# Split SiLU-multiply on one core: the first tile's store in four pieces, and no copy ahead of the third load

## The chip, the cores and the metric

The kernel runs on one core of a Trainium2 chip. Its time is device time in microseconds (us), as the median of several runs; less is better. Beside the times there is one profiled execution with a trace of every instruction and every DMA packet. The engines that matter here are ScalarE (ACT), VectorE (DVE), SyncE (SP, which only issues transfers) and the core's 16 DMA engines, which move data between HBM and the on-chip memory (SBUF, 128 partitions).

## The reference

```python
batch, seq, dim = (32, 512, 2048)          # x: float32
half_dim = x.shape[-1] // 2
x1, x2 = x[..., :half_dim], x[..., half_dim:]
silu_x1 = x1 * (1 / (1 + np.exp(-x1)))
return (silu_x1 * x2).astype(np.float32)   # (32, 512, 1024)
```

Each of the 16384 rows of 2048 numbers becomes one row of 1024: SiLU of the left half times the right half. 134 MB are read and 67 MB written.

## The kernel before

The 16384 rows are cut into 16 tiles of 1024 rows. A tile gives each of the 128 partitions `K` = 8 neighbouring rows, so a partition's share of a load is 64 KB in one stretch of HBM, and its share of a store is 32 KB. The input tiles `xt` and the output tiles `ot` come from pools with two buffers each: tile i + 2 has the buffers of tile i.

One tile is worked on in four chunks of `KC` = 2 rows. For each chunk ACT writes SiLU of the left half to `ot` (line 87), and DVE multiplies `ot` in place by the right half (line 92).

The schedule is written out by hand, so each engine does its instructions in program order:

- ACT issues the loads (line 74) as well as computing. Loads 0 and 1 come first (the first one is moved ahead of the opening barrier). After the four chunks of tile i ACT issues load i + 2, which waits until ACT and DVE have read tile i, since it overwrites that buffer. Tile i + 1's activations stand behind that load in ACT's queue.
- SP issues the stores. Tiles 0 to 14 are stored whole, when their last multiply is done (line 100). The last tile, 15, is stored in four pieces of two rows, each when its multiply is done (line 98).
- DVE does the multiplies, and once, after tile 0, a copy of one row of `xt` onto itself (line 103). Load 2 overwrites that buffer, so it waits for the copy too, while the store of tile 0 only waits for the last multiply.

An activation of tile i + 2 writes to the buffer that the store of tile i reads, so it waits for that store. The program's framework places the semaphores for these waits.

Of the kernel before, what the change touches and what calls it, by code (L numbers as in the profile page):

```python
# [1 line left out]

# [4 lines left out]


def issue_ahead_of_the_first_barrier(nc):

    head, body = nc.main_func.blocks[:2]
    load = next(ins for ins in body.instructions if type(ins).__name__ == "InstDMACopy")
    at = next(
        j for j, ins in enumerate(head.instructions)
        if ins.engine == load.engine and type(ins).__name__ == "InstDrain"
    )
    body.instructions = [ins for ins in body.instructions if ins.name != load.name]  # L20
    head.instructions = head.instructions[:at] + [load] + head.instructions[at:]


@with_exitstack
def kernel(
    ctx: ExitStack,
    tc: tile.TileContext,
    x: bass.AP,
    out: bass.AP,
):  # L30

    nc = tc.nc
    P = nc.NUM_PARTITIONS

    x_flat = x.flatten_outer_dims()  # L40
    out_flat = out.flatten_outer_dims()
    num_rows, in_cols = x_flat.shape
    half = in_cols // 2
    dt = x_flat.dtype

    K = 8
    KC = 2
    PLAN = [K] * (num_rows // (P * K))

    in_pool = ctx.enter_context(tc.tile_pool(name="in_pool", bufs=2))  # L50
    out_pool = ctx.enter_context(tc.tile_pool(name="out_pool", bufs=2))

    plan = []
    row = 0
    for k in PLAN:
        plan.append((row, k))
        row += P * k
    assert row == num_rows
    n_tiles = len(plan)

    def view(flat, i):
        row0, k = plan[i]
        return flat[row0:row0 + P * k].rearrange("(p k) d -> p k d", k=k)

    nc.at_finalize(issue_ahead_of_the_first_barrier)


    ctx.enter_context(tc.manual_schedule())

    loaded = {}  # L70

    def load(i):
        xt = in_pool.tile([P, K, in_cols], dt, name="xt")
        nc.scalar.dma_start(out=xt[:, :plan[i][1], :], in_=view(x_flat, i))
        loaded[i] = xt

    load(0)
    load(1)
    for i in range(n_tiles):
        k = plan[i][1]  # L80
        xt = loaded.pop(i)
        last = i == n_tiles - 1
        ov = view(out_flat, i)
        ot = out_pool.tile([P, K, half], dt, name="ot")
        for c in range(0, k, KC):
            ce = min(c + KC, k)
            nc.scalar.activation(  # L87
                out=ot[:, c:ce, :],
                in_=xt[:, c:ce, :half],
                func=mybir.ActivationFunctionType.Silu,  # L90
            )
            nc.vector.tensor_mul(  # L92
                out=ot[:, c:ce, :],
                in0=ot[:, c:ce, :],
                in1=xt[:, c:ce, half:],
            )
            if last:
                nc.sync.dma_start(out=ov[:, c:ce, :], in_=ot[:, c:ce, :])
        if not last:
            nc.sync.dma_start(out=ov, in_=ot[:, :k, :])  # L100
        if i == 0:

            nc.vector.tensor_copy(out=xt[:, k - 1, :half], in_=xt[:, k - 1, :half])  # L103
        if i + 2 < n_tiles:
            load(i + 2)


# [1 line left out]
_INS = ['x']  # L109
_OUTS = [((32, 512, 1024), 'float32')]  # L110


# [23 lines left out]
```

## Time and profile before

| | us |
|---|---|
| median of 3 runs | 470.83 (470.68 to 471.1) |
| the profiled execution: its time | 470.83 |
| the profiled execution: its span | 469.0 |
| DVE busy (64 multiplies and the copy) | 142.9 |
| ACT busy (64 activations, a table load) | 118.2 |

The span is the stretch that the instructions cover; 1.8 us of the time lie around it. Of a profile's lines: a group reads "line, engine, operation, written tile <- read tiles, shape, how many"; in the list by time the first number is the start in us from the span's start, the second the length, and brackets hold how long the engine had been idle and what ended that. `ACTq`, `DVEq` and `SPq` are the engines' issuing sides, at which semaphore waits and transfers stand. In the row of 40 slices, one digit is the busy share of 11.7 us in tenths. q10 is the queue of ACT's transfers (the loads), q1 that of SP's (the stores).

### The profile page before, as it was taken

To read this page: it belongs to the slowest core of one execution; us is meant where nothing else is said; L and a number is where in the kernel's file an instruction comes from. 1 tells how busy PE (TensorE), PEld (TensorE's weight loads), DVE (VectorE), ACT (ScalarE), POOL (GpSimd) and SP (SyncE) were. 2 spreads that over 40 slices of the span, in tenths; PEclk is the share of its full clock that TensorE was granted. 3 is DMA by queue.
4 is the path that set the end of the run, shared out by engine and by line. 5 is a ranking of instruction groups with operands and counts; after the bars stand their busy time and mean duration, and the time that the engine had idled before them with its cause. 6 is when DMAs were issued, how large, how long until landed. Compare 5 with 4: busy or idle time off the path is not lost.

```text
span 469.0 us, 271 instructions
## 1 busy us (share of the span) xinstructions
DVE 142.9 (30%) x65; ACT 118.2 (25%) x65; POOL 0.2 (0%) x4
## 2 busy tenths in 40 slices
DVE  0080705207051060611606015070250702407033
ACT  1151406014060230602306032060420604106050
POOL 0000000000000000000000000000000000000000
DMA  9899999999999998999999999999999999999998
GB/s 425 386 442 402 436 458 442 408 411 439 447 447 402 444 472 380 447 481 397 464 400 430 467 442 408 408 442 447 447 402 442 464 391 447 439 433 469 397 413 353
DMA packets 5042, 201.35 MB, mean 429 GB/s; under 512 B 560, under 2 KB 560, under 8 KB 560
## 3 DMA queue, kind: packets, MB, share of 16 engines
q10 hardware_dynamic: 2304, 134.22, 66.4%
q1 hardware_dynamic: 2736, 67.11, 33.2%
q14 instruction: 2, 0.02, 0.0%
HBM read 134.22 MB, written 67.11 MB: 429 GB/s over the span
## 4 chain that ended last, share of the span: by engine, by line
DMA 80%; DVE 15%; ACT 3%; DVEq 0%; issue 0%
DMA xt<-in_x_dram 80%; DVE ot L92 15%; ACT ot L87 3%; DVEq L131 0%
## 5 line engine op out<-in xcount | busy, mean ns | idle before, releaser
L92 DVE TENSOR_TENSOR ot<-ot,xt 128x2048 f32<-128x2048 f32 x64 | 142.3, 2286 | 319.1 <-ACT ot L87 319.1
L87 ACT ACTIVATE ot<-xt 128x2048 f32<-128x2048 f32 x64 | 116.9, 1897 | 339.0 <-DMA xt<-in_x_dram 339.0
L87 ACT ACT_TABLE_LOAD x1 | 1.3, 1283 | 1.3 <-PEq L120 1.3
L103 DVE COPY xt<-xt 128x1024 f32<-128x1024 f32 x1 | 0.7, 683 | 0.0
L120 POOL MEMSET const-bfloat16-1.0<- 128x1 bf16 x1 | 0.1, 101 | 0.0
L120 POOL MEMSET const-uint8-127<- 128x1 uint8 x1 | 0.1, 101 | 0.0
L120 POOL MEMSET const-float32-0.0<- 128x1 f32 x1 | 0.1, 98 | 0.2 <-issue 0.2
L120 POOL MEMSET const-float32-1.0<- 128x1 f32 x1 | 0.1, 98 | 0.0
## 6 DMA issues: line engine op xcount, KB each, us to landing
out_dram<-ot SPq DMA_DIRECT2D x15, 4096.0 KB, 39.7
out_dram<-ot SPq DMA_DIRECT2D x4, 1024.0 KB, 5.7
xt<-in_x_dram ACTq DMA_DIRECT2D x16, 47.1
```

What stands on the lines that cost most here:

```text
L87: nc.scalar.activation(out=ot[:, c:ce, :], in_=xt[:, c:ce, :half], func=mybir.ActivationFunctionType.Silu,)
L92: nc.vector.tensor_mul(out=ot[:, c:ce, :], in0=ot[:, c:ce, :], in1=xt[:, c:ce, half:],)
L103: nc.vector.tensor_copy(out=xt[:, k - 1, :half], in_=xt[:, k - 1, :half])
L120: nc = _bacc.Bacc("TRN2", target_bir_lowering=False, num_devices=1)
```

## The change

The first tile is now stored like the last one: each two-row piece as soon as its multiply is done. The copy on DVE is gone, so load 2 waits for tile 0's last multiply alone. Nothing else differs.

```diff
     for i in range(n_tiles):
         k = plan[i][1]
         xt = loaded.pop(i)
-        last = i == n_tiles - 1
+        in_pieces = i in (0, n_tiles - 1)
         ov = view(out_flat, i)
         ot = out_pool.tile([P, K, half], dt, name="ot")
         for c in range(0, k, KC):
...
-            if last:
+            if in_pieces:
                 nc.sync.dma_start(out=ov[:, c:ce, :], in_=ot[:, c:ce, :])
-        if not last:
+        if not in_pieces:
             nc.sync.dma_start(out=ov, in_=ot[:, :k, :])
-        if i == 0:
-
-            nc.vector.tensor_copy(out=xt[:, k - 1, :half], in_=xt[:, k - 1, :half])
         if i + 2 < n_tiles:
             load(i + 2)
```

## The prediction

> **What bounds the kernel now.** I read the page first (slices, queues, chain), then the issues with their landing times, then the start in order of time, and last the packet records behind section 3.
>
> ```profile
> DMA  9899999999999998999999999999999999999998
> q10 hardware_dynamic: 2304, 134.22, 66.4%
> q1 hardware_dynamic: 2736, 67.11, 33.2%
> DMA 80%; DVE 15%; ACT 3%; DVEq 0%; issue 0%
> out_dram<-ot SPq DMA_DIRECT2D x15, 4096.0 KB, 39.7
> out_dram<-ot SPq DMA_DIRECT2D x4, 1024.0 KB, 5.7
> xt<-in_x_dram ACTq DMA_DIRECT2D x16, 47.1
> ```
>
> The 16 DMA engines are busy in every slice, and the loads (q10) and stores (q1) together take 66.4% + 33.2% = 99.6% of their time. The chain names loads, DVE and ACT in turn, but each of its steps only issues a transfer into engines that are full already. So the time is the sum of the packets, plus any moment in which both queues are empty.
>
> The packet records say what one engine does. A load gives each engine eight packets of 64 KB at 2418 ns and a completion; a whole store gives eight of 32 KB at 1213 ns; a piece of a store (the last tile's four) gives eight of 8 KB at 309 ns. Check: 128 × 2.418 + 120 × 1.213 + 32 × 0.309 = 465.0 us. The first packet starts 1.13 us into the span, the first store costs 1.2 us once (below), the last completion and the closing barrier take about 1.2 us: 468.5 of the 469.0.
>
> Two more things stand in the records. While both queues hold work, an engine takes one packet of each in turn, whatever their sizes: 64 KB, 32 KB, 64 KB, 32 KB, from 39 us to the last load. A completion takes a turn of its own. And the end is only just covered: the last load's data is in at 448.65 on the first engine, seven packets of store 14 follow until 457.14, and the last tile's first piece starts there, at 457.13, having been issued at 455.43.
>
> ```profile
> 22.07 7.31 ACT L87 ACTIVATE ot<-xt 128x2048 f32<-128x2048 f32 x4 [19.50 <-DMA xt<-in_x_dram]
> 24.01 8.89 DVE L92 TENSOR_TENSOR ot<-ot,xt 128x2048 f32<-128x2048 f32 x4 [24.01 <-ACT ot L87]
> 32.82 0.68 DVE L103 COPY xt<-xt 128x1024 f32<-128x1024 f32 x1
> 32.93 23.61 SPq L100 DMA_DIRECT2D out_dram<-ot  x2
> 33.60 0.33 ACTq L74 DMA_DIRECT2D xt<-in_x_dram  x1
> 45.34 7.31 ACT L87 ACTIVATE ot<-xt 128x2048 f32<-128x2048 f32 x4 [15.97 <-DMA xt<-in_x_dram]
> 47.28 8.90 DVE L92 TENSOR_TENSOR ot<-ot,xt 128x2048 f32<-128x2048 f32 x4 [13.78 <-ACT ot L87]
> 56.21 0.37 ACTq L74 DMA_DIRECT2D xt<-in_x_dram  x1
> ```
>
> From a landing to the issue of the load two tiles on, 10.87 us pass (45.34 to 56.21): one activation, then four multiplies.
>
> ```profile
> L87 ACTq EVENT_SEMAPHORE  x14: 17/17/17, 74.1 to 443.9; - x14
> ```
>
> This is ACT's wait for the output buffer: one for each tile from tile 2 on, ahead of its first activation, for the store two tiles back. It costs nothing now, as that store lands 7 us earlier.
>
> **The copy.** L103 takes 0.68 us of DVE and holds load 2 from 32.95 to 33.60. Load 1's packets run until 43.47, and load 2 stands behind them in the same queue. So its earlier issue is worth 0; without that cover it would be worth 0.65 us. Tile 1's activations, behind load 2 in ACT's queue, wait for their data until 45.34 in any case.
>
> **Four pieces: their own cost.** 32 packets of 309 ns (9.89 us) take the place of eight of 1213 ns (9.70): +0.2 us on a full engine. The three added issues take 0.33 us each on SP, which otherwise waits for DVE; behind them stands only store 1, due at about 55. DMA semaphores come round again after eight transfers (12 waits of 17 ns at L100); with three more transfers load 4 meets one of a piece, which tile 2 has waited for by then anyway.
>
> The Trainium skill (DMA: Bandwidth & Descriptors, "Anatomy of one DMA — SWDGE (gpsimd) path") gives a fixed cost of about 2.0 us to a DMA. By that, three more would add an estimated 6 us. These stores are issued by SP, though, and the last tile's four pieces run back to back: 32 × 0.309 = 9.9 us, and their packets start between 457.13 and 467.48. The measurement decides: no fixed cost on queued transfers.
>
> **Four pieces: the turns.** Here I see the price. Packets of 8 KB that alternate with 64 KB ones make the store slow and the loads fast.
> - Piece 0 is issued at 24.01 + 2.28 = 26.29, not 32.93. Before, a store issued at 32.93 started at 39.01: the packet in flight and one more load packet went ahead, the latter stretched from 2.42 to about 3.6 us. The same from 26.29: load packets of 25.79 and 28.20 go ahead, first store packet at 28.20 + 2.42 + 1.2 = 31.8.
> - Store 0 needs 32 + 4 completions = 36 turns. The loads have 4 packets of load 1 left, 8 each of loads 2 and 3, and 3 completions: 23 turns. They end at 31.8 + 20 × 2.418 + 23 × 0.309 = 87.3. Load 2 has landed at 65.7 then (74.16 before), load 1 at about 44.
> - Store 0's other 13 turns run alone, 4 us: its last data is out at about 91.2. Store 1 follows, 8 × 1.213 = 9.7 us, to 100.9.
> - Tile 2 has the buffer that store 0 reads. If its first activation waits for all of store 0, as the single wait ahead of each tile suggests, it starts at 91.2 + 0.8 = 92.0 (a completion follows an engine's data by 0.35 to 1.2 us). Load 4 is issued 10.87 later, at 102.9, and the first packet comes 1.0 to 2.1 us after (load 0: issued at 0.13, packets at 1.13 to 2.13), say 104.4. Tile 3 and load 5 stand behind this in ACT's queue, store 2 in SP's.
> - Between 100.9 and 104.4 both queues are empty: 3.5 us. A refill from nothing costs another 0.4 (at the start the second round came 2.9 us after the first, not 2.42).
>
> From there load 4 and store 2 run side by side for 29 us as before, and store 14 is whole when the last load lands, so the end is covered better than now. Sum: 0.2 + 3.5 + 0.4 = 4.1. With the ends of the rows (landing 0.35 to 1.2, first packet 1.0 to 2.1, refill 0 to 0.8) the gap is 2.5 to 5.3 and the sum 2.7 to 5.5. The profiled execution took 470.83, its span and 1.8 us around it, which is also the median: 474.9, within 473.5 to 476.3.
>
> **Rivals.**
> 1. *ACT waits piece by piece.* Each activation then needs only the piece that it overwrites. The fourth still waits until 92.0, but then one activation and one multiply follow (1.92 + 2.28): load 4 at 96.2, its packets by 98.3, before store 1 runs out at 100.9. No gap, +0.2: 471.0. For it: the stores are cut by rows. Against it: one wait ahead of each tile; but the trace before has no buffer in pieces that is used again. 0.17.
> 2. *Two to four 8 KB packets in a turn.* Store 0 then needs 20 or 12 turns, is done before load 3, and nothing stalls: 471.0. Against it: the strict one-to-one. No row shows 8 KB beside 64 KB. 0.08.
> 3. *The stores get ahead.* If turns went by bytes, or a piece's eight packets went as one turn, store 0 would end two packets earlier against the loads than now, and so every store after. The end has no slack: with two packets (2.4 us) less of store 14, the engines wait for the last tile's first piece. +2.5, 473.3 by bytes; about +1.1, 471.9, by eight. 0.12.
> 4. *Faster.* The 1.2 us that the first store costs could vanish when small packets join the loads; only then, and with no gap anywhere, is it 0.2 - 1.2 = -1.0: 469.8. It decides only without the wait of tile 2. The page has nothing else to gain, as the same bytes go through full engines. 0.08.
>
> The Trainium skill (DMA: Bandwidth & Descriptors, "Queues, rings and completion order") has engines change queues only at packet ends, with typically 9 to 17 descriptors in a packet. If a record here were one descriptor and a piece's eight made one packet, this would speak for rival 3's lower figure; the records show single 64 KB and 32 KB blocks taking turns, and none of 8 KB beside loads.
>
> **How the numbers follow.** The gap at tile 2 has 0.55: its arithmetic needs one-to-one turns, which the records show for 400 us, and a wait for the whole buffer, which they suggest. With rival 3 (0.12) that is 0.67 slower; rivals 1 and 2 make 0.25 for no change, rival 4 0.08 for faster. "No change" is within 0.2%, 0.94 us, about what a measurement of this kernel can tell. The range runs from rival 1 and 2, less 0.4 for the first store's cost, to the upper end of the gap: 470.6 to 476.3.
>
> **What would show it.** Right: load 2 lands near 66 and load 3 near 88; tile 2's first activation waits for a store until about 92; load 4 is issued near 103; DMA share and GB/s drop in the slice from 94 to 105; store 0's last piece takes 55 to 60 us from issue to landing. If ACT's tile 2 is spread out instead, rival 1 holds. If load 2 lands at 74 or later, turns are not one-to-one: rivals 2 or 3, told apart by whether the last load's landing leaves a hole before the first piece of tile 15. I am wrong altogether if the DMA engines show a hole elsewhere, or if packets of 8 KB beside loads take much more than 309 ns.

## The result, and the profile after

| | before | after |
|---|---|---|
| median of 4 runs, us | 470.87 (470.68 to 471.1) | 474.91 (474.82 to 475.25) |
| the profiled execution, us | 470.83 | 475.25 |
| its span, us | 469.0 | 473.5 |

The ratio is 1.0087, with a 95% interval of 1.0069 to 1.0104. By medians the change costs 4.04 us; the two profiled spans are 4.4 apart, as the profiled execution after is the slowest of its four.

The slices, queues and issues of the page after:

```profile
DMA  9999998979999999999999999999999999999988
GB/s 415 421 426 410 476 421 388 435 285 407 435 487 399 432 415 482 399 443 465 421 399 443 487 399 399 443 482 404 418 424 487 399 435 435 460 399 440 473 374 352
q10 hardware_dynamic: 2304, 134.22, 65.9%
q1 hardware_dynamic: 3168, 67.11, 33.1%
out_dram<-ot SPq DMA_DIRECT2D x14, 4096.0 KB, 46.9
out_dram<-ot SPq DMA_DIRECT2D x8, 1024.0 KB, 16.8
```

The DMA row shows a 7 in the ninth slice (95 to 106 us), and the row below falls to 285 GB/s there (411 before). Averaged over the span, the two queues' shares fall only from 99.6% to 99.0%: most of the loss is one hole, a stretch in which both queues are empty, and the slice finds it.

The start in order of time:

```profile
26.26 6.94 SPq L98 DMA_DIRECT2D out_dram<-ot  x4
32.87 0.37 ACTq L74 DMA_DIRECT2D xt<-in_x_dram  x1
43.44 7.31 ACT L87 ACTIVATE ot<-xt 128x2048 f32<-128x2048 f32 x4 [14.13 <-DMA xt<-in_x_dram]
54.31 0.37 ACTq L74 DMA_DIRECT2D xt<-in_x_dram  x1
90.76 7.31 ACT L87 ACTIVATE ot<-xt 128x2048 f32<-128x2048 f32 x4 [40.01 <-DMA out_dram<-ot]
92.70 8.90 DVE L92 TENSOR_TENSOR ot<-ot,xt 128x2048 f32<-128x2048 f32 x4 [38.42 <-ACT ot L87]
101.62 0.37 ACTq L74 DMA_DIRECT2D xt<-in_x_dram  x1
```

Loads 1 to 3 land early (43.4, 65.3 and 87.3), and then tile 2's four activations together start only at 90.76, released by a store (`out_dram<-ot`) and no longer by a load. Load 4 is issued at 101.62. Before, these two stood here:

```profile
74.16 7.31 ACT L87 ACTIVATE ot<-xt 128x2048 f32<-128x2048 f32 x4 [21.51 <-DMA xt<-in_x_dram]
85.03 0.37 ACTq L74 DMA_DIRECT2D xt<-in_x_dram  x1
```

ACT's semaphore waits after, and its total of waiting, say the same:

```profile
L87 ACTq EVENT_SEMAPHORE  x15: 17/17/22929, 65.3 to 453.3; - x15
ACT ot L87 <- DMA out_dram<-ot: 40.0, 1, 40.0
```

Before, each of these waits took 17 ns; now one takes 22.9 us: from 65.3, when load 2's data was there, to 88.2, when the third piece landed; the rest, to 90.7, went to the last piece. The 40.0 us of the second line are all of ACT's idle time before tile 2, the wait for load 2 included.

The packet records show the turns. Store 0's first 8 KB packet starts at 30.82, after the fourth packet of load 1, and from there each engine takes 8 KB and 64 KB packets in turn, one of each, until load 3 ends at 85.9 to 86.6, depending on the engine. Then the other 8 KB packets run back to back until 89.7 to 90.3, and store 1's eight of 32 KB until 99.2 to 100.0. The next packets start at 102.45 to 102.60.

### The profile page after: what moved, and what is told of

It reads as the page before. It is cut to its first block, busy times and chain, and to the rows that moved or that the text cites. A ratio compares the mean times of both kernels' runs of the same rounds, so it can differ in the third digit from the quotient of the medians.

```text
span 473.5 us, 276 instructions
## 1 busy us (share of the span) xinstructions
DVE 142.3 (30%) x64; ACT 118.2 (25%) x65; POOL 0.2 (0%) x4
## 4 chain that ended last, share of the span: by engine, by line
DMA 69%; DVE 16%; another core or an unknown queue 8%; ACT 4%; DVEq 0%; issue 0%; ACTq 0%
DMA xt<-in_x_dram 69%; DVE ot L92 16%; ACT ot L87 4%; DVEq L128 0%; ACTq L74 0%; ACTq L87 0%
```

## The experiments

Four readings had to be told apart: the turns with the wait for the whole buffer (the forecast), the early start of the store, the number of transfers, and the copy. Ratios are against runs of the kernel before on the same chip. The code cuts show the edit against the kernel after the change; only the first one is against the kernel before.

**One half alone: no copy, first tile whole.**

```diff
-        if i == 0:
-            nc.vector.tensor_copy(out=xt[:, k - 1, :half], in_=xt[:, k - 1, :half])
```

> Half of the change alone: the first tile is stored whole as before, only the copy is gone. Turns theory (8 KB packets take turns one to one with 64 KB ones, so store 0 outlasts load 3, and tile 2, which waits for all of store 0, issues load 4 too late): the copy has no part in it, as load 2 stands behind load 1 until 43.5 us anyway; no change against before, within 0.3 us of it, DMA engines full throughout. Rival, the copy's order mattered (load 2 issued together with the store hurts the store): some or all of the 4.0 us shows here, 472 to 475.

470.97 us, ratio 0.9993 (0.9985 to 1.0002). Load 2 is issued 0.8 us earlier, at 32.82, but load 1, which runs ahead of it, lands only at 44.8 (45.3 before). The copy is worth nothing that can be measured.

**The other half alone: four pieces, with the copy.**

```diff
+        if i == 0:
+            nc.vector.tensor_copy(out=xt[:, k - 1, :half], in_=xt[:, k - 1, :half])
```

> The other half of the change alone: four pieces, and the copy stays. Turns theory: the copy holds load 2 for 0.65 us, behind which load 1 still runs; 474.9 as the change, within 0.3. Rival, the copy matters once the pieces are there (it held load 2 back and gave the store turns): 471 to 474.

474.90 us, ratio 1.0078 (1.0063 to 1.0093): with the copy kept, the pieces bring the cost by themselves.

**Two pieces of four rows.**

```diff
-            if in_pieces:
+            if i == n_tiles - 1:
                 nc.sync.dma_start(out=ov[:, c:ce, :], in_=ot[:, c:ce, :])
+            elif i == 0 and ce in (4, 8):
+                a = max([0] + [e for e in (4, 8) if e < ce])
+                nc.sync.dma_start(out=ov[:, a:ce, :], in_=ot[:, a:ce, :])
```

> The first tile in two pieces of 4 rows (16 KB packets) instead of four of 2 rows, no copy. Turns theory: store 0 needs 16 + 2 = 18 turns and the loads offer 23, so it is done near 80 us, while load 3 still runs; no hole, 0 to 0.8 us under before (the packet lengths that the first store stretches may shrink, as they did with four pieces), so 470.0 to 470.9. Rival, each added transfer costs about 1.35 us (4.0 over three): +1.35, 472.2. Rival, the early start of the store costs: piece 1 starts only 2 us later than with 2-row pieces, so most of +4 stays, 474.

470.87 us, ratio 0.9996 (0.9987 to 1.0005). From its list by time:

```profile
82.66 7.31 ACT L87 ACTIVATE ot<-xt 128x2048 f32<-128x2048 f32 x4 [29.03 <-DMA out_dram<-ot]
93.54 0.36 ACTq L74 DMA_DIRECT2D xt<-in_x_dram  x1
```

Tile 2 waits for store 0 here as well, 8.5 us longer than before the change. But load 3 lands only at 97.3, so load 4 is queued behind a load that still runs, and the wait is free. (In the profiled execution, of 472.15 us, the 16 DMA engines end up to 2.0 us apart, against 0.85 before.)

**Three pieces, of two, two and four rows.** The same edit with `(2, 4, 8)` for `(4, 8)` in both places.

> The first tile in three pieces of 2, 2 and 4 rows (8, 8 and 16 KB packets), no copy. Turns theory: 24 + 3 = 27 turns against 23 of the loads, so store 0 still outlasts load 3 (done near 90 us) and the hole stays whole, about 3 us between 98.5 and 102 and a refill: 474.5 to 475. Rival, each added transfer costs 1.35 us: 2.7, 473.5. A price that grows evenly with the number of small packets would be two thirds, 473.5, as well.

475.05 us, ratio 1.0082 (1.0068 to 1.0096). Again the list by time:

```profile
90.53 7.31 ACT L87 ACTIVATE ot<-xt 128x2048 f32<-128x2048 f32 x4 [39.90 <-DMA out_dram<-ot]
101.40 0.37 ACTq L74 DMA_DIRECT2D xt<-in_x_dram  x1
```

The cost is a step. With 18 turns of store 0 it is nothing, with 27 the whole 4 us, with 36 the same. The loads offer 22 or 23 turns, and the step lies between 18 and 27. A price for each transfer would have given a third for every piece.

**Late pieces, first attempt: the four stores written behind tile 0's last multiply.**

> Four pieces of 2 rows as in the change, but all four issued after the first tile's last multiply, when the whole store was issued before; no copy. Turns theory: the start is late but the turns are as many: 36 against 20 that the loads offer from 39 us on, so store 0 is done near 90 us again and the hole stays: 474.5 to 475.3. Rival, the early start costs (stores competing with load 1): nothing is early here, so 470.9 to 471.2.

474.99 us, ratio 1.0082 (1.0068 to 1.0096), but it tells nothing new: SP was idle and each store waits for its own multiply only, so it issued them from 26.37 on, as in the change.

**Late pieces, second attempt: the last rows' piece first.** All four then stand behind the last multiply.

```diff
+        if i == 0:
+            for c in range(k - KC, -1, -KC):
+                nc.sync.dma_start(out=ov[:, c:c + KC, :], in_=ot[:, c:c + KC, :])
```

> Four pieces of 2 rows, with the last rows' piece issued first, so that all four stand behind the last multiply on SP and none is issued before about 32.9 us; no copy. Turns theory: the start is late but the turns are as many: 36 against 20 that the loads offer from 39 us on, so store 0 is done near 90 us again and the hole stays: 474.5 to 475.3. Rival, the early start costs: 470.9 to 471.2.

475.33 us, ratio 1.0095 (1.0074 to 1.0116):

```profile
33.04 1.95 SPq L101 DMA_DIRECT2D out_dram<-ot  x4
90.91 7.31 ACT L87 ACTIVATE ot<-xt 128x2048 f32<-128x2048 f32 x4 [40.77 <-DMA out_dram<-ot]
```

Issued 6.8 us later, store 0 is done at the same time (its last data lands at 90.8, in the change at 90.7), though load 3 lands 0.8 us earlier. Until then the engines are full in both kernels, with the same loads 1 to 3 and the same store 0. The early start is not the cause.

**Load 3 held back.** The pieces and the wait stay, but DVE copies tile 1's left halves onto themselves three times, and load 3 waits for that.

```diff
+        if i == 1:
+            for _ in range(3):
+                nc.vector.tensor_copy(out=xt[:, :, :half], in_=xt[:, :, :half])
```

> The change as it is, pieces and waits for the whole buffer, but load 3 is issued later: DVE copies tile 1's left halves onto themselves three times (3 x about 5.5 us) after its last multiply, and load 3 waits for that, until about 71 us in place of 54.3. Turns theory: with no load to alternate with after load 2 (data in near 64), store 0's last 23 turns run alone in 7 us and it lands near 72 in place of 90; tile 2 is then through near 83 and load 4 is issued while load 3 runs: no hole, 470.8 to 472, although a load is held back for 16 us. Rival, the pieces cost by themselves (small packets, more transfers) or the hole comes from anything but loads outrunning store 0: 475 or more.

471.05 us, ratio 1.0006 (0.9997 to 1.0016):

```profile
54.27 13.34 DVE L103 COPY xt<-xt 128x8192 f32<-128x8192 f32 x3
67.71 0.34 ACTq L74 DMA_DIRECT2D xt<-in_x_dram  x1
71.80 7.31 ACT L87 ACTIVATE ot<-xt 128x2048 f32<-128x2048 f32 x4 [20.97 <-DMA out_dram<-ot]
82.67 0.37 ACTq L74 DMA_DIRECT2D xt<-in_x_dram  x1
```

13 us of added work and a load issued 13.4 us later save 3.9 us. When load 2 has ended, nothing takes turns with store 0's small packets, so they run alone; tile 2 starts 19 us earlier than in the change, and load 4 finds load 3 still running. So neither the small packets nor the wait cost the time by themselves, but loads that outran the store.

**Waits by rows.** Pieces as in the change; both output buffers are one tile that is never given back, so each activation of tile 2 waits for its own piece.

```diff
+    both = out_pool.tile([P, 2 * K, half], dt, name="ot")   # pool with bufs=1
...
-        ot = out_pool.tile([P, K, half], dt, name="ot")
+        ot = both[:, (i % 2) * K:(i % 2 + 1) * K, :]
```

> The change as it is (four pieces, no copy), but the two output buffers are one tile that is never given back, so each activation of tile 2 waits only for the piece of store 0 that it overwrites. Turns theory: store 0 is as slow as in the change (last piece landed near 90 us), but only tile 2's fourth activation waits for it; load 4 is issued near 95 in place of 101.6, before store 1 runs out near 100, so there is no hole: 470.5 to 471.3, with loads 2 and 3 still landing early (65, 88). Rival, the slow store itself or the small packets cost the time, whatever waits for it: 474.9 as in the change.

479.21 us, ratio 1.0167 (1.0152 to 1.0183): both theories missed. Its list by time, and its load queue:

```profile
65.55 1.91 ACT L88 ACTIVATE ot<-xt 128x2048 f32<-128x2048 f32 x1 [14.67 <-DMA xt<-in_x_dram]
73.65 1.91 ACT L88 ACTIVATE ot<-xt 128x2048 f32<-128x2048 f32 x1 [6.18 <-DMA out_dram<-ot]
88.19 1.91 ACT L88 ACTIVATE ot<-xt 128x2048 f32<-128x2048 f32 x1 [12.63 <-DMA out_dram<-ot]
90.65 1.91 ACT L88 ACTIVATE ot<-xt 128x2048 f32<-128x2048 f32 x1 [0.55 <-DMA out_dram<-ot]
94.92 0.37 ACTq L75 DMA_DIRECT2D xt<-in_x_dram  x1
q10 hardware_dynamic: 2304, 134.22, 66.5%
```

The part that was meant works. Tile 2 is spread over its pieces, load 4 is issued 6.7 us earlier than in the change, and the packet records have no hole there. But the loads' packets now take 317.5 us of each engine, and before the change 311.2: 6.3 us more for the same packets. Most of what is left of the 8.4 us between the two profiled spans is idle time at the end, 1.7 us more than before, since the engines now finish up to 3.7 us apart, against 0.85. In every period from tile 4 on, some packets of the load that has just begun are stretched, by some 0.5 us in all, averaged over the engines. And each load lands about 3.5 us, one round of packets, before a store (load 4 at 130.1, store 2 at 133.5).

**What stretches the packets?** Two kernels with the single output tile, but another first tile: whole, and in two pieces of four rows.

> The output buffers as one tile that is never given back, as in the run with waits by rows, but the first tile stored whole and no copy. There the hole was gone and the time was 479 all the same, with load packets stretched by some 0.5 us around every tile. Theory A, the single output tile itself (its place or its waits) stretches packets: it does so here too, 475 to 479. Theory B, the stretching belongs to the order of transfers that the pieces leave behind (in each period a load ends about one packet before a store): here the order is that of before, so 470.7 to 471.3 and no stretched packets after 40 us.

> The single output tile with waits by rows, and the first tile in two pieces of 4 rows. Store 0 is done near 81 us before load 3, so there is no hole, and tile 2's first two activations start before its last two. Theory A (the single tile stretches packets): 475 to 479. Theory B (only an order of transfers in which a load ends just before a store does): 470.7 to 471.5, unless this start leads into that order.

470.81 us (0.9994, 0.9985 to 1.0004) and 470.89 us (0.9998, 0.9989 to 1.0007), with no stretched packets after 41 us worth counting. So it is neither the single tile nor its waits.

Then the kernel with waits by rows, with one DVE copy after tile 2 that holds load 4 back, of six rows and of two:

```diff
+        if i == 2:
+            nc.vector.tensor_copy(out=xt[:, :6, :half], in_=xt[:, :6, :half])   # or :2
```

> The kernel with pieces and waits by rows (479.2 us), with one DVE copy of six rows (about 3.3 us) after tile 2's last multiply, which holds load 4 until about 98 us; store 2 is issued at 95 as before. Order theory (the stretched packets come from the order in which each load ends about one packet round ahead of a store): load 4 then starts beside or behind store 2, the two ends fall differently in every period after, and the stretching goes: 470.9 to 472.5, though a load is held back. Rival, the stretching comes from the waits by rows or from store 0's pieces as such: 478 to 483.

> The same with a copy of two rows (about 1.1 us): load 4 is issued near 96, still more than 3 us before store 1 runs out, and starts ahead of store 2 as before. Order theory: the same order in each period as without the copy, stretched packets around each tile, 478 to 480; if only the exact time within a round mattered, 471 to 475.

472.04 us (1.002, 1.001 to 1.0029) and 472.68 us (1.004, 1.0018 to 1.0062), the latter spread from 471.02 to 475.21. In the first, the stretching is gone from 140 us on. What it still costs lies elsewhere: its engines idle for 1.2 us between 457 and 459. Store 14 runs out there as early as before the change, but the last load lands 2.8 us later, and the first piece of tile 15 is issued only at 458.22 (455.43 before). That is the hole of the prediction's rival 3, reached in another way. The second expectation failed in its premise. It had load 4 start ahead of store 2, as it does without the copy (99.56 and 105.08); in the profiled execution, the one of 471.02, store 2 began one packet ahead of load 4 (99.39 and 100.62), and from then on the two end together (129.8 and 129.9), with no stretching. So in these profiles the stretching goes with the order in which loads and stores end, and 1.2 us of delay can change that order. Why this order stretches packets stays open, and so does whether this kernel's executions of up to 475.21 us were in it: they have no profile.

No kernel here beats the one before: the five with neither a hole nor the stretching (no copy, two pieces, load 3 held back, and the two with the single output tile and another first tile) lie between 470.81 and 471.05, all within 0.1% of it.

## Why the prediction was right

The main case's forecast was 474.9 us, within 473.5 to 476.3; measured were 474.91. Its mechanism held at each step. That the two numbers meet to 0.01 us is luck all the same: several terms were off, in opposite directions.

- **The copy: 0.** Measured alone, 470.97 against 471.12.
- **The turns.** On the engine that is first, the first store packet was foreseen at 31.8 and found at 30.8; the end of the loads 87.3 and 85.9; store 0's last data 91.2 and 89.7. Tile 2's start was foreseen at 92.0 and found at 90.76, load 4's issue 102.9 and 101.62. 1.0 us of the lead is the first store, which did not stretch the packet before it to 3.6 us this time (2.43 to 2.69). Another 1.2 us is a slip in the sum: it gives each of store 0's 36 turns 309 ns, but four of them are completions, which take 9 ns in the records. Load packets stretched later on take back 0.6. Both ends of the hole moved nearly as far, so this hardly touched the time.
- **The wait for the whole buffer.** Rival 1 falls: all four activations waited for the last piece. (The semaphore that load 4 met again was load 1's and not a piece's; that cost nothing.) Its price for waits by rows, 471.0, was wrong too, by the stretching, a cost of which the trace before has no sign.
- **The hole: 3.5 foreseen, 3.0 found.** The engines are idle for 3.6 us on average after the start, against 0.6 before. The step that was too large is the first packet after the restart: I took load 4's, 1.5 us after its issue, but store 2 is issued in the same moment, and its first packet starts 0.8 us after (102.45).
- **The refill: 0.4 foreseen, 1.5 found.** Store 2's first packet took 1.83 to 2.02 us in place of 1.21, load 4's first 2.98 to 3.41 in place of 2.42.
- **The first store's cost: left as it was, found 0.4 lower.** Before it stretches load packets by 1.06 us, after by 0.63 over several places.
- **Sum of the profiled pair:** idle +3.0, stretch beyond the usual packet lengths +1.3 (refill 1.5, first store -0.4, small ones), smaller packets +0.2: 4.5, and the spans differ by 4.4. Foreseen were 4.1.
- **Rivals 2 and 3** fall with the records: one 8 KB packet in each turn, and store 0 done after load 3. **Rival 4** had a grain of truth: part of the first store's cost did go. But alone it brings no measurable gain: two pieces, without a hole, took 470.87.

The Trainium skill (DMA: Bandwidth & Descriptors, "Queues, rings and completion order") says that an engine changes queues only at the ends of packets. This trace agrees, if each of its records is such a packet: while both queues held work, the engines changed over after every single block of 8 or 64 KB. The page's typical 9 to 17 descriptors in a packet would have let a piece's eight blocks go as one, were a block one descriptor; that did not happen. The page's fixed cost of about 2.0 us for each DMA ("Anatomy of one DMA — SWDGE (gpsimd) path"), which it gives for transfers issued by the gpsimd engine, shows nowhere as added time in these stores, which SP issues: one transfer more cost nothing in the two-piece kernel (470.87 us, against 471.12).

## What to carry to other kernels

When two queues take turns packet by packet, the sizes of their packets set the shares: here a store cut into 8 KB packets beside loads of 64 KB got an eighth of the loads' rate, and all that waited for its buffer waited with it. Count turns, not bytes: the cost is a step, from nothing to all, at the point where the slow transfer outlasts the loads that are already queued. This kernel, at 99.6% of its transfer time, had nothing to gain from finer pieces at its start, where nothing is waiting for the store to begin: two pieces changed nothing, three and four cost 4 us.

## What the hardware showed unexpectedly

- A transfer that joined busy engines came behind several packets of the other queue, and not behind one: about four store packets of 32 KB ahead of load 4 in the kernel with waits by rows (issued at 94.92, first packet at 99.56), and two load packets of 64 KB ahead of the first store before the change (issued at 32.93, first packet at 39.01).
- The restart from empty queues cost 1.5 us in stretched packets, beyond the idle time.
- With an order of transfers in which each load ends one packet round before a store came 6 us of stretched load packets over the run; the same transfers in another order (the profiled execution of 471.02 us) had none of it. What links the two is open.
